# A two-layer encoder trunk in FP32 on one core: order of the down projection's loads, two banks for a broadcast, two remainders on VectorE

## Chip, cores and metric

The kernel runs on one core of a Trainium2 chip. The metric is the device time of one execution in microseconds (us); lower is better. The core has five engines with instruction streams of their own: PE (TensorE, matmuls; PEld is its weight loading), DVE (VectorE), ACT (ScalarE), POOL (GpSimd) and SP (SyncE, which here issues nearly all DMA transfers). SBUF is the on-chip memory, PSUM holds the matmuls' results in eight banks.

## The reference

The input is 1024 tokens by 1024 features. Layer 0 is an mLSTM mixer and a SwiGLU, layer 1 is chunked attention and a SwiGLU, and an RMSNorm ends it. The change touches only the two SwiGLU blocks and the last norm:

```python
def rmsnorm(x, g):
    y = x32 * lax.rsqrt(jnp.mean(x32 * x32, axis=-1, keepdims=True) + EPS) * g.astype(jnp.float32)

def swiglu(h, w_gate, w_up, w_down):
    return (jax.nn.silu(h @ w_gate) * (h @ w_up)) @ w_down
...
x = x + swiglu(rmsnorm(x, g), w_gate, w_up, w_down)
```

The hidden size of the SwiGLU is 2816, that is 22 blocks of 128. All of it is in FP32.

## The kernel before

**Precision.** Each FP32 operand is split into a high part, which ACT casts, and a remainder, which DVE or POOL subtracts (operand minus high part). A block product is three matmuls: high by high, remainder by high, high by remainder. So an operand is of use to PE only when load, cast and subtraction are done, in this order.

**Gate and up projections** (`gate_up`, product at L989). They use a Strassen-Winograd scheme: per unit n (a pair of 128-wide blocks of the gate or of the up weights) seven products a, b, c, d of sums of blocks. For each unit the weights are loaded to `wr`, DVE makes the sums s1 and s2 (L954, L959) and POOL s3 and s4 (L955, L960). `wc{layer}{n}_{c}` is the split weight of product c; its high part is L965 (ACT), its remainder L967, on POOL for unit 0 and for product 0 of unit 1, on DVE elsewhere. The input is multiplied in before its norm is known. The norm's sum of squares is built beside it: L309 adds squares into `f_s`, L316 sums over partitions on PE (`f_ps`), L278 to L285 take the reciprocal root on DVE, L332 in `finish_b` broadcasts it over the partitions on PE in two halves of four matmuls (`f_pb0`, `f_pb4`), and ACT copies each half to `f_rbc` (L341). The first results are multiplied by it (L1004, L1006, L1008) before Silu (L1007). Eight PSUM banks are split in one `mx` bank and seven `pj` banks that the products use.

**Down projection** (`down`, product at L1261, L1262 in the changed file). Seven sums i = 0 to 6 (b11, b21, t4, t3, t2, n1, b22) of the gated hidden state, stored in device memory by `gate_up`, are multiplied by four output blocks u: 28 products of 33 matmuls with 512 columns, in the order (0,0), (0,1), (0,2), (0,3), (1,0) and so on. In layer 1 the last sum is done in two halves of 256 columns (at = 0, 1). `fetch(i, k)` loads operand k of sum i through an `hr` slot (L1134, six slots) and splits it to `hc` (L174 on ACT, L175 on DVE). `prepare(i, u)` splits the weight to `wc` (two slots); for sum 0 the weight comes in three pieces `wd{layer}first...` through the same `hr` slots (L1157), for the other sums from tiles `wd` loaded whole (`wload`, L1128, 704 KB each) or combined from two of them (L1143 to L1149). The residual blocks h0 to h7 (512 KB each, L1238, L1247) are read back for `settle` (L1198 to L1222), which adds the products up. In layer 1 `scale_out` (L1184 to L1190) multiplies the finished half or quarter of the output by the last norm's factor and stores it; `fin_ps`, `fin_pb` and `fin_rbc` are that norm's sum, broadcast and copy.

**What sets the order.** The kernel is written in program order, and the order within each engine's stream follows from it and from the priorities of the operations: each engine then works its stream strictly in order. SP issues the loads in order as well; an issue waits for its slot, and for the load eight places earlier to have landed. The lines of the down projection that set the loads are these:

```python
need = [("w", 0, 0, 0)] + [("x", 0, k) for k in range(NP)] + [("w", 0, 1, 0)]
...
for u in range(NU):
    nc.sync.dma_start(h[u], mixed.kept[u])
    wload(u, 0, 1)
```

## Time and profile before

| what | us |
|---|---|
| median of 3 runs | 2446.05 |
| lowest and highest run | 2440.4, 2451.39 |
| the profiled execution, its own time | 2446.85 |
| its span in the trace | 2445.1 |
| PE busy (share of the span) | 2332.5 (95%) |
| DVE, POOL, ACT busy | 1706.7 (70%), 1029.2 (42%), 975.9 (40%) |

The span is the time between the first and the last event that the trace shows on the core; 1.75 us of the profiled execution lie outside it. Busy times are averages over stages with different limits. In brackets behind a row of a timeline stands the idle time of the engine before it, and the work that ended this idle time.

### The profile page before, as it was taken

The page shows a single profiled execution, that of the slowest core. Times are in us where ns is not written, and L with a number is a line of the kernel's source. Part 1 is how long each engine was busy: PE and PEld are TensorE (multiplying, and loading weights), DVE is VectorE, ACT ScalarE, POOL GpSimd, SP SyncE. Part 2 cuts the span into 40 slices and gives each one's busy share as a digit, 9 for nine tenths or more (in the row PEclk, how much of TensorE's full clock was granted, in tenths as well). Part 3 has the DMA queues.
Part 4 walks back from the last instruction along what each step waited for, and adds up shares of the span by engine and source line. Part 5 has one row for each costly group of instructions (what it writes and reads, how often), then busy time and mean ns, then how long its engine had stood idle before and what let it go on. Part 6 is the DMA issues. An engine that isn't in the chain of part 4 may idle for free. (4 is left out here: it accounts for less than half of the span.)

```text
span 2445.1 us, 31222 instructions
## 1 busy us (share of the span) xinstructions
PE 2332.5 (95%) x11568; PEld 1929.3 (79%) x11568; DVE 1706.7 (70%) x2699; ACT 975.9 (40%) x1826; POOL 1029.2 (42%) x644
## 2 busy tenths in 40 slices
PE   8999999989999997999999999989889999997997
PEld 7888787777888886888878787868677888876877
DVE  6544455887777765797377777787887777764887
ACT  5322222442332323544366666655533322333444
POOL 2000000476666661122664545350776666640142
PEclk9999999989999998999999999999999999998999
DMA  3110102312223227542111111001312232239431
GB/s 135 44 35 26 44 19 86 131 67 104 101 94 116 100 103 291 205 142 76 53 45 39 37 38 40 32 23 45 122 70 98 96 129 91 104 124 355 159 124 52
DMA packets 91017, 232.00 MB, mean 95 GB/s; under 512 B 10096, under 2 KB 13424, under 8 KB 90864
## 3 DMA queue, kind: packets, MB, share of 16 engines
q1 hardware_dynamic: 89136, 227.91, 26.9%
q8 instruction: 90, 1.47, 0.3%
q10 hardware_dynamic: 1728, 2.10, 0.2%
q14 instruction: 63, 0.52, 0.1%
HBM read 177.01 MB, written 52.95 MB: 94 GB/s over the span
## 5 line engine op out<-in xcount | busy, mean ns | idle before, releaser
L1261 PE MATMUL dn<-hc,wc 128*128 128x512 f32 (+1 forms) x1980 | 432.7, 380 | 27.3 <-ACT wc L174 23.9
L1261 PEld LDWEIGHTS dn<-hc,wc 128*128 128x128 f32 x1980 | 357.0, 190 | 101.8 <-ACT wc L174 24.7
L989 PE MATMUL a<-b,wc 128*128 128x512 f32 x1056 | 261.6, 398 | 8.2 <-POOL wc L967 4.2
L989 PE MATMUL c<-t,wc 128*128 128x512 f32 x1056 | 257.6, 393 | 6.2 <-DVE c L1062 6.2
L989 PEld LDWEIGHTS a<-b,wc 128*128 128x128 f32 x1056 | 201.9, 191 | 55.0 <-ACT wc L965 4.9
L989 PEld LDWEIGHTS c<-t,wc 128*128 128x128 f32 x1056 | 199.2, 189 | 51.1 <-DVE c L1062 7.5
L967 DVE TENSOR_TENSOR wc<-s,wc 128x512 fp32r<-128x512 f32 x168 | 181.4, 1081 | 68.5 <-ACT wc L965 67.3
L965 ACT CAST wc<-s 128x512 fp32r<-128x512 f32 x176 | 107.7, 619 | 183.6 <-PE d L989 111.6
L730 POOL TENSOR_TENSOR hv<-num 128x1024 f32<-128x1024 f32 x8 | 15.2, 1895 | 342.4 <-ACT num L706 342.4
L174 ACT CAST wc<-wd 128x512 fp32r<-128x512 f32 x156 | 82.0, 582 | 141.4 <-PE dn L1261 132.0
L989 PE MATMUL b<-t,wc 128*128 128x512 f32 x528 | 131.6, 399 | 6.1 <-POOL wc L967 6.1
L175 DVE TENSOR_TENSOR hc<-hr,hc 128x512 fp32r<-128x512 f32 x154 | 105.3, 728 | 36.7 <-ACT hc L174 36.6
L989 PE MATMUL d<-b,wc 128*128 128x512 f32 x528 | 131.0, 397 | 0.0
L965 ACT CAST wc<-wr 128x512 fp32r<-128x512 f32 x132 | 80.5, 618 | 125.7 <-PE c L989 42.6
L989 PE MATMUL d<-n,wc 128*128 128x512 f32 x528 | 130.6, 396 | 0.0
L967 DVE TENSOR_TENSOR wc<-wr,wc 128x512 fp32r<-128x512 f32 x124 | 113.0, 912 | 20.0 <-ACT wc L965 20.0
L1400 ACT ACTIVATE p<-p,mn 128x640 f32<-128x640 f32 (+4 forms) x128 | 89.2, 697 | 87.8 <-DVE mn L1389 80.9
L989 PEld LDWEIGHTS b<-t,wc 128*128 128x128 f32 x528 | 100.7, 191 | 29.1 <-POOL wc L967 7.0
L174 ACT CAST hc<-hr 128x512 fp32r<-128x512 f32 x154 | 89.4, 617 | 72.4 <-DMA hr<-kb 53.2
L989 PEld LDWEIGHTS d<-b,wc 128*128 128x128 f32 x528 | 99.3, 188 | 24.1
L989 PEld LDWEIGHTS d<-n,wc 128*128 128x128 f32 x528 | 100.2, 191 | 21.7
L1022 POOL TENSOR_TENSOR c<-c,c 128x512 f32<-128x512 f32 x44 | 73.1, 1662 | 104.2 <-DVE c L1066 89.9
(817 smaller groups left out, 5828.2 us busy)
## 6 DMA issues: line engine op xcount, KB each, us to landing
wd<-in_w_down_dram SPq DMA_DIRECT2D x40, 704.0 KB, 7.8
wr<-in_w_gate_dram SPq DMA_DIRECT2D x44, 512.0 KB, 4.4
wr<-in_w_up_dram SPq DMA_DIRECT2D x44, 512.0 KB, 4.3
kb<-c SPq DMA_DIRECT2D x66, 256.0 KB, 2.3
kt<-t SPq DMA_DIRECT2D x66, 256.0 KB, 2.0
hr<-kb SPq DMA_DIRECT2D x66, 256.0 KB, 4.0
hr<-kt SPq DMA_DIRECT2D x66, 256.0 KB, 3.9
hd<-h SPq DMA_DIRECT2D x16, 512.0 KB, 2.7
```

Of the source, the lines that this page charges most:

```text
L174: nc.scalar.copy(hi, src)
L175: nc.vector.tensor_tensor(lo, src, hi, ALU.subtract)
L730: nc.gpsimd.tensor_tensor(x, nv, nv, ALU.mult)
L965: hi = nc.scalar.copy(t[:, 0:HT], src)
L967: eng.tensor_tensor(t[:, HT:T], src, t[:, 0:HT], ALU.subtract)
L989: nc.tensor.matmul(ps, a, b, start=(first and k == 0 and i == 0), stop=(k == len(xs) - 1 and i == 2), skip_group_check=True,)
L1022: nc.gpsimd.tensor_tensor(x, x, g, ALU.mult)
L1261: nc.tensor.matmul(ps, a, b, start=(k == 0 and j == 0), stop=(k == NP - 1 and j == 2))
L1400: nc.scalar.activation(p, p, AF.Exp, bias=mnv, scale=-1.0, accum_out=sm)
```

## The change

It has four parts.

1. In `finish_b` the second half of the broadcast takes a `pj` bank, where the first half has the `mx` bank (when the tiles are pinned, which is so in `gate_up`).
2. The remainders of products 0 and 1 of unit 0 are subtracted on DVE, not on POOL.
3. In `down` only blocks u = 0 and 1 of sum 0 load their weights in pieces. Blocks 2 and 3 are loaded whole, once, right behind the second piece load; these tiles serve later sums too, so that two loads of 704 KB per layer fall away. The loads of h0 to h3 and of the tiles (u,0,1) move from ahead of the products into the products of sum 0, and those of h4 to h7, of (u,1,1) and of the tiles (0,0,0) and (1,0,0) into those of sum 1.
4. In layer 1 the scaling of the finished first half of the output moves from behind product (4,3) to behind (5,0), and that of the next quarter from behind (6,3) of the first half to behind the first product of the second half.

```diff
@@ -327,7 +327,7 @@
             t0, nt = cols.start // P, (cols.stop - cols.start) // P
             for i0 in range(0, nt, 4):
                 n = min(4, nt - i0)
-                pb = mxt(f"{self.name}_pb{t0 + i0}")
+                pb = (pjt if pin and i0 else mxt)(f"{self.name}_pb{t0 + i0}")
                 for i in range(n):
                     mm = nc.tensor.matmul(
                         pb[:, i * P : (i + 1) * P],
@@ -963,7 +963,7 @@
             src = (a11, s2, s3, s1, a12, a22, s4)[c]
             t = full("hl", f"wc{layer}{n}_{c}", F32R)
             hi = nc.scalar.copy(t[:, 0:HT], src)
-            eng = nc.gpsimd if n == 0 or (n, c) == (1, 0) else nc.vector
+            eng = nc.gpsimd if n == 0 and c > 1 or (n, c) == (1, 0) else nc.vector
             eng.tensor_tensor(t[:, HT:T], src, t[:, 0:HT], ALU.subtract)
             ready[n, c] = t
             return hi
@@ -1152,7 +1152,7 @@
             t = pools["wc"].tile([P, 2, WC], F32R, tag="wc", name=f"wc{layer}{i}{u}{at}")
             block = ((0, 0), (0, 1), (1, 1), (1, 0), (1, 0), (0, 0), (0, 1))[i]
             for c, n in pieces:
-                if i == 0:
+                if i == 0 and u < 2:
                     src = hrt(f"wd{layer}first{u}{c}")[:, 0:n]
                     nc.sync.dma_start(src, wsrc(u, 0, 0)[:, c : c + n])
                 else:
@@ -1228,26 +1228,27 @@
         order = [(i, u, 0) for i in range(len(names)) for u in range(NU)]
         if last:
             order += [(i, u, 1) for i, u, _ in order[-NU:]]
-        need = [("w", 0, 0, 0)] + [("x", 0, k) for k in range(NP)] + [("w", 0, 1, 0)]
-        for step in need:
-            (prepare if step[0] == "w" else fetch)(*step[1:])
+        prepare(0, 0)
+        for k in range(NP):
+            fetch(0, k)
+        prepare(0, 1)
+        for u in (2, 3):
+            wload(u, 0, 0)
         for e in range(NK):
-            ht = coret(f"hr{layer}_{e}")
-            h.append(ht)
-        for u in range(NU):
-            nc.sync.dma_start(h[u], mixed.kept[u])
-            wload(u, 0, 1)
+            h.append(coret(f"hr{layer}_{e}"))
         for m, (i, u, at) in enumerate(order):
             if m + 2 < len(order) and order[m + 2][2] == 0:
                 combine(*order[m + 2][:2])
             if m + 1 < len(order) and order[m + 1] not in wcs:
                 prepare(*order[m + 1])
             if i == 0:
-                wload(u, 0, 0)
+                wload(u, 0, 1)
+                nc.sync.dma_start(h[u], mixed.kept[u])
+            if i == 1:
                 nc.sync.dma_start(h[u + NU], mixed.kept[u + NU])
-            if i == 0 and u >= 2:
-                for v_ in (2 * u - 4, 2 * u - 3):
-                    wload(v_, 1, 1)
+                wload(u, 1, 1)
+                if u >= 2:
+                    wload(u - 2, 0, 0)
             if i == 2:
                 wload(u, 1, 0)
             w = wcs.pop((i, u, at))
@@ -1267,12 +1268,12 @@
             if i == 4:
                 wload(u, 0, 1)
             settle(i, u, at, n, ps)
-            if last and u == NU - 1:
-                if i == 4:
-                    r_fin.append(coret("fin_rbc"))
-                    scale_out(hs(0))
-                if i == 6:
-                    scale_out(slice(HT + at * n, HT + at * n + n))
+            if last and (i, u) == (5, 0):
+                r_fin.append(coret("fin_rbc"))
+                scale_out(hs(0))
+            if last and (i, u, at) in ((6, 0, 1), (6, NU - 1, 1)):
+                c = HT if u == 0 else HT + n
+                scale_out(slice(c, c + n))
         sb.close()
         return xs, st
 
```

The order on the engines at the places concerned follows. First SP at the start of the down projection of layer 1, before, from the last store of the hidden state that is needed first; `hr1_e` is residual block e, `hr11_k` operand k of sum 1, `wd1uij` a whole weight tile of block u, `wd1first2...` the pieces of block 2:

```order
L1013 DMA kt4_110_19148<-t41_10_19137 128x512
L1238 DMA hr1_1_19259<-hd11_15467 128x1024
L1238 DMA hr1_2_19260<-hd12_15570 128x1024
L1128 DMA wd1001_19267<-in_w_down_dram 128x1408
L1128 DMA wd1101_19270<-in_w_down_dram 128x1408
L1128 DMA wd1201_19273<-in_w_down_dram 128x1408
L1238 DMA hr1_3_19261<-hd13_15754 128x1024
L1128 DMA wd1301_19276<-in_w_down_dram 128x1408
L1128 DMA wd1000_19278<-in_w_down_dram 128x1408
L1247 DMA hr1_4_19262<-hd14_15889 128x1024
L1134 DMA hr11_0_19315<-kb21_10_16144 128x512
L1134 DMA hr11_1_19320<-kb21_11_16450 128x512
```

The same place after the change:

```order
L1013 DMA kt4_110_19136<-t41_10_19125 128x512
L1134 DMA hr11_0_19295<-kb21_10_16132 128x512
L1134 DMA hr11_1_19300<-kb21_11_16438 128x512
L1134 DMA hr11_2_19352<-kb21_12_16738 128x512
L1128 DMA wd1200_19246<-in_w_down_dram 128x1408
L1128 DMA wd1300_19248<-in_w_down_dram 128x1408
L1128 DMA wd1001_19258<-in_w_down_dram 128x1408
L1128 DMA wd1101_19315<-in_w_down_dram 128x1408
L1246 DMA hr1_1_19251<-hd11_15455 128x1024
L1134 DMA hr11_3_19357<-kb21_13_17038 128x512
L1128 DMA wd1201_19372<-in_w_down_dram 128x1408
L1246 DMA hr1_2_19252<-hd12_15558 128x1024
```

The operands of sum 1 and the whole tiles of blocks 2 and 3 now stand directly behind the stores, ahead of residual blocks 1 to 4 and of the tiles (u,0,1); the pieces of block 2 are gone.

PE in the gate and up projections of layer 0, where the norm's factor is broadcast (`f0_pb0` and `f0_pb4` are the two halves, `d00` and `d01` products of the two column halves), as a difference:

```order
 L332 MATMUL f0_pb0_4202<-packed_58,f00_y_4064 128x128 x4
+L332 MATMUL f0_pb4_4208<-packed_58,f00_y_4064 128x128 x4
 L989 MATMUL d01_4217<-n1_00_3630,wc01_3_4111 128x512 x3
 L989 MATMUL d01_4217<-n1_01_3733,wc01_3_4111 128x512 x3
-L989 MATMUL d01_4217<-n1_02_3836,wc01_3_4111 128x512
-L332 MATMUL f0_pb4_4208<-packed_58,f00_y_4064 128x128 x4
-L989 MATMUL d01_4217<-n1_02_3836,wc01_3_4111 128x512 x2
+L989 MATMUL d01_4217<-n1_02_3836,wc01_3_4111 128x512 x3
```

The second half of the broadcast moved up by seven matmuls, directly behind the first.

DVE at the start of the gate and up projections of layer 0, two pieces of the difference (`wc00_0` and `wc00_1` are the split weights of products 0 and 1 of unit 0):

```order
 L833 TENSOR_TENSOR h1_7_3471<-h1_7_3471,wb7_p0_3882 128x512
 L833 TENSOR_TENSOR h1_7_3471<-h1_7_3471,wb7_p1_3899 128x512
+L967 TENSOR_TENSOR wc00_0_3952<-wr00_3946,wc00_0_3952 128x512
 L898 SCALAR_TENSOR_TENSOR n1_03_3962<-h1_3_3183,packed_58,xg03_3955 128x512
 L954 TENSOR_TENSOR s1_00_3982<-wr00_3946 128x512
...
 L881 TENSOR_TENSOR t3_03_3969<-xg03_3955,t3_03_3969 128x512
 L954 TENSOR_TENSOR s1_01_4008<-wr01_3949 128x512
+L967 TENSOR_TENSOR wc00_1_3990<-s2_00_3986,wc00_1_3990 128x512
 L959 TENSOR_TENSOR s2_01_4012<-s1_01_4008,wr01_3949 128x512
 L178 SCALAR_TENSOR_TENSOR b21_00_4098<-h1_4_3244,packed_58,b21_00_4098 128x512
```

The first remainder stands ahead of the input's last block, the second between the sums s1 and s2 of unit 1. Further on in the same stream the sum s1 of unit 2 moved behind the last t4, b21 and b22 of the input.

PE at the end of the down projection of layer 1, around the last norm's first half, before (`dn1500` is product (5,0)):

```order
L1261 MATMUL dn1500_20545<-hc15_4_20397,wc1500_20410 128x512 x3
L1261 MATMUL dn1500_20545<-hc15_5_20453,wc1500_20410 128x512 x2
L316 MATMUL fin_ps0_20491<-ones_59,fin_s_19176 128x1 x4
L1261 MATMUL dn1500_20545<-hc15_5_20453,wc1500_20410 128x512
L1261 MATMUL dn1500_20545<-hc15_6_20458,wc1500_20410 128x512 x3
L1261 MATMUL dn1500_20545<-hc15_7_20463,wc1500_20410 128x512 x3
L1261 MATMUL dn1500_20545<-hc15_8_20468,wc1500_20410 128x512 x3
L332 MATMUL fin_pb0_20512<-packed_58,fin0_y_20500 128x128 x4
L1261 MATMUL dn1500_20545<-hc15_9_20473,wc1500_20410 128x512 x3
```

And after the change (`dn1510` is product (5,1)):

```order
L1262 MATMUL dn1500_20474<-hc15_10_20454,wc1500_20386 128x512 x3
L316 MATMUL fin_ps0_20523<-ones_59,fin_s_19164 128x1 x4
L1262 MATMUL dn1510_20577<-hc15_0_20251,wc1510_20467 128x512 x3
...
L1262 MATMUL dn1510_20577<-hc15_6_20434,wc1510_20467 128x512 x3
L332 MATMUL fin_pb0_20544<-packed_58,fin0_y_20532 128x128 x4
L1262 MATMUL dn1510_20577<-hc15_7_20439,wc1510_20467 128x512 x3
```

The sum moved from within product (5,0) to its end, and the broadcast from there into (5,1).

## Rows read from the trace of the kernel before

**Rows 1.** The profile's page: its first line, and of its list of the costliest groups the matmuls of the down projection (line engine op out<-in xcount | busy us, mean ns of one | idle us of the engine just before them, what ended most of it).
```profile
span 2445.1 us, 31222 instructions
...
L1261 PE MATMUL dn<-hc,wc 128*128 128x512 f32 (+1 forms) x1980 | 432.7, 380 | 27.3 <-ACT wc L174 23.9
```

**Rows 2.** The timeline of PE (TensorE) at the start of the down projection of layer 1 (two rows) and of layer 0 (two rows). Columns: start us, us, engine line op out<-in, form, count, and in brackets the idle time before and what ended it. The windows end at 2260 and 1000 us, so the second row of each pair goes on behind them.
```profile
2195.22 15.16 PE L1261 MATMUL dn<-hc,wc 128*128 128x512 f32 x65 [1.15 <-DVE wc L175]
2222.72 37.55 PE L1261 MATMUL dn<-hc,wc 128*128 128x512 f32 x151 [12.33 <-ACT wc L174]
...
937.58 15.18 PE L1261 MATMUL dn<-hc,wc 128*128 128x512 f32 x65 [1.15 <-DVE wc L175]
964.29 35.90 PE L1261 MATMUL dn<-hc,wc 128*128 128x512 f32 x146 [11.53 <-ACT wc L174]
```

**Rows 3.** Windows at the same two places, in the order layer 1 (three rows) and layer 0 (two): window, length, busy us and count of PE, PEld, DVE, ACT and POOL, PE's granted clock (1.00 is full speed), busy share of the DMA engines, GB/s.
```profile
2210.40:2222.70 12.30, 0.00 (x0) 0.00 (x0) 2.06 (x4) 2.46 (x5) 0.00 (x0) 0.67 1.02 408
2222.70:2226.00 3.30, 3.28 (x7) 2.36 (x8) 1.79 (x3) 1.01 (x2) 0.00 (x0) 0.50 1.02 396
2226.00:2230.00 4.00, 4.00 (x14) 3.15 (x14) 2.42 (x4) 2.90 (x5) 0.00 (x0) 0.72 1.04 402
964.30:968.00 3.70, 3.70 (x8) 2.68 (x9) 1.77 (x3) 0.99 (x2) 0.00 (x0) 0.50 1.01 392
968.00:972.00 4.00, 4.00 (x17) 3.21 (x17) 2.24 (x4) 2.69 (x5) 0.00 (x0) 0.91 1.06 406
```

**Rows 4.** The timeline of SP's DMA issues at the start of the down projection of layer 1 (start us, us of issuing, line, destination<-source, count). hd are the kept residual blocks, kb the stored sums of the gated hidden state, wd and wd1first weights.
```profile
2201.84 0.88 SPq L1238 DMA_DIRECT2D hr<-hd  x2
2202.77 1.40 SPq L1128 DMA_DIRECT2D wd<-in_w_down_dram  x3
...
2204.80 1.06 SPq L1128 DMA_DIRECT2D wd<-in_w_down_dram  x2
2206.12 0.53 SPq L1247 DMA_DIRECT2D hr<-hd  x1
2208.21 2.60 SPq L1134 DMA_DIRECT2D hr<-kb  x2
2212.23 3.35 SPq L1157 DMA_DIRECT2D wd1first<-in_w_down_dram  x3
```

**Rows 5.** The timelines of ACT (two rows) and of DVE (one row) in the same stretch.
```profile
2220.64 1.30 ACT L174 CAST hc<-hr 128x512 fp32r<-128x512 f32 x2 [9.63 <-DMA hr<-kb]
2222.05 1.66 ACT L174 CAST wc<-wd1first 128x512 fp32r<-128x512 f32 x3
...
2200.17 2.85 DVE L175 TENSOR_TENSOR wc<-wd1first,wc 128x512 fp32r<-128x512 f32 x3
```

**Rows 6.** The list of DMA issues in the window 2160 to 2300 us: destination<-source, queue, count, KB each, median us from issue to landing.
```profile
wd<-in_w_down_dram SPq DMA_DIRECT2D x16, 704.0 KB, 8.4
...
hr<-kb SPq DMA_DIRECT2D x22, 256.0 KB, 4.7
```

**Rows 7.** The timeline of PE in the gate and up projections: layer 0 (four rows), layer 1 (two rows).
```profile
489.06 7.94 PE L989 MATMUL a<-b,wc 128*128 128x512 f32 x23 [2.08 <-POOL wc L967]
...
499.93 4.10 PE L989 MATMUL b<-t,wc 128*128 128x512 f32 x11 [2.70 <-POOL wc L967]
...
524.88 2.08 PE L332 MATMUL f_pb<-packed,f_y 128*128 128x128 f32 x8 [5.28 <-ACT f_rbc L341]
...
562.10 4.14 PE L989 MATMUL c<-t,wc 128*128 128x512 f32 x10 [2.92 <-DVE c L1062]
...
1782.10 2.08 PE L332 MATMUL f_pb<-packed,f_y 128*128 128x128 f32 x8 [5.33 <-ACT f_rbc L341]
...
1820.04 3.04 PE L989 MATMUL c<-t,wc 128*128 128x512 f32 x12 [2.58 <-DVE c L1062]
```

**Rows 8.** The timelines of POOL (two rows), DVE (three) and ACT (one) at the start of the gate and up projections of layer 0.
```profile
498.62 1.25 POOL L967 TENSOR_TENSOR wc<-s,wc 128x512 fp32r<-128x512 f32 x1
...
529.11 1.75 POOL L1004 TENSOR_TENSOR c<-c,f_rbc 128x512 f32<-128x512 f32 x1
...
499.90 0.69 DVE L959 TENSOR_TENSOR s<-s,wr 128x512 f32<-128x512 f32 x1 [2.37 <-POOL wc L967]
...
510.60 0.69 DVE L967 TENSOR_TENSOR wc<-wr,wc 128x512 fp32r<-128x512 f32 x1
...
527.92 1.77 DVE L959 TENSOR_TENSOR s<-s,wr 128x512 f32<-128x512 f32 x1
...
527.24 0.57 ACT L341 COPY f_rbc<-f_pb 128x512 f32<-128x512 f32 x1
```

**Rows 9.** One window of the gate and up projections of layer 0, columns as in the windows above.
```profile
530.00:540.00 10.00, 10.00 (x45) 8.13 (x45) 9.78 (x10) 3.85 (x7) 9.92 (x7) 1.00 0.07 28
```

**Rows 10.** The timelines of PE (four rows) and of DVE (one) at the end of the down projection of layer 1. fin_ps and fin_pb are the sums and the broadcast of the last norm.
```profile
2367.26 1.02 PE L316 MATMUL fin_ps<-ones,fin_s 128*128 128x1 f32 x8 [1.70 <-DVE fin_s L309]
2368.15 4.13 PE L1261 MATMUL dn<-hc,wc 128*128 128x512 f32 x10
...
2383.50 32.47 PE L1261 MATMUL dn<-hc,wc 128*128 128x512 f32 x212 [1.17 <-DVE wc L175]
...
2421.07 0.68 PE L332 MATMUL fin_pb<-packed,fin_y 128*128 128x128 f32 x4 [0.60 <-DVE fin_y L285]
...
2373.82 6.63 DVE L1187 SCALAR_TENSOR_TENSOR hr<-hr,packed,fin_rbc 128x512 f32<-128x512 f32 x5 [2.34 <-ACT fin_rbc L341]
```

## The prediction

> **What bounds the kernel now.** I read the page first, then PE's timeline for its idle places, then at each place the streams of the engine or queue that ended the wait. PE is the bound over the whole span; its idle time is small and sits in a few places. Of 27.3 us of idle time in the down projection, 23.9 lie in two waits ended by the cast of a weight [rows 1]: 12.33 us in layer 1 and 11.53 in layer 0, each two products after the start, where block 2 of sum 0 is due [rows 2]. In the wait PE runs nothing and the DMA engines run full at 408 GB/s [rows 3]. SP shows why: three residual blocks and five whole weight tiles go out before the first operand of sum 1 at 2208.21 and the pieces of block 2 at 2212.23 [rows 4], and ACT casts what it had waited for only at 2220.64 and 2222.05 [rows 5]. So this is an order of loads, not a lack of DMA rate: the tiles sent first are wanted only from sum 1 on. After each wait PE's granted clock is .50 and then .72 (layer 1) or .91 (layer 0) before it is full again [rows 3]: .50 of 2.4 GHz is the lower of its two levels, and what came before was an idle PE.
>
> **Part 3, the down projection.** Removed are the two waits and what the clock costs behind them. Layer 1: 3.3 us at .50 and 4.0 at .72 lose 3.3 x .50 + 4.0 x .28 = 2.8 us; layer 0: 3.7 x .50 + 4.0 x .09 = 2.2 [rows 3]. Together 12.33 + 2.8 + 11.53 + 2.2 = 28.9 us [rows 2, 3].
>
> What is late next? After the change three operands (256 KB each) and then the tile of block 2 (704 KB) go out at about 2201.8, when the residual blocks went out before [rows 4]. With the last stores in flight I take 1.77 MB ahead of and including that tile: 1.77 MB / .398 MB per us (between the rates of 396 and 408 in rows 3) is 4.4 us, and 1.4 us for issue and landing make 2207.6. The first third of the weight then needs a cast (1.66 us for three [rows 5], .6 for one) and a subtraction (.69 [rows 8]): 2208.9. Block 2 is due at the end of product (0,1), 2210.4 [rows 2]. So no wait by 1.5 us, which is thin. The other end is what the first operand of sum 1 took in this very place, issued at 2208.21 and cast at 2220.64, 12.4 us [rows 4, 5]: a tile issued at 2201.8 would land at 2214.2, be ready at 2215.6, and PE would wait 5.2 us and lose about 1 on its clock, 6.3 per layer. I take 1 us per layer, near the lower end, because the 12.4 us had over 5 MB ahead of them (five tiles and three residual blocks sent in the 4.3 us before [rows 4]), and medians in this stretch are 8.4 us for such a tile and 4.7 for an operand [rows 6].
>
> Sum 1 is next. A product of 33 matmuls is 7.6 us (two of them, but for the first matmul, take 15.16 [rows 2]), so sum 0 ends at about 2225.5 and the last operand of (1,0) is due at 2232.4. By then 9.04 MB must be in (1.77, and behind them five tiles, three residual blocks and eight operands): 22.7 us at .398 from 2201.8, plus 2.7 for landing and splitting, give 2227.2; slack 5 us. It fails only below some .32 MB per us, and the lowest rate in rows 3 is .39. The two tiles that are saved (1.44 MB) are 3.6 us of queue in the same stretch. Residual blocks 1 to 3 are behind them; `settle` wants them on ACT and DVE, not on PE, and with six `pj` banks a late one has some products of cover. Blocks 4 to 7 now wait for an SBUF slot that an operand of sum 0 holds until about 2225.5, and SP's whole queue waits with the first of them; behind it are the operands of sum 2, due at 2255.8. Cover 30 us, price nothing unless that slot comes free much later (rival 4). Net: 28.9 - 2 = **26.9 us**, bounds 16.3 and 28.9.
>
> **Part 4, the tail.** PE waits 1.70 us for the last addition of the statistics, runs ten matmuls in 4.13 us where rows 2 give .233 each (2.3 us), so 1.8 on the clock, waits 1.17 for a weight's remainder that DVE makes behind 6.63 us of scaling, and .60 at the quarter [rows 10]; 5.3 us in all. The sum moved behind the whole product has 5 us more cover. The scaling now lies in product (5,1) or later and can push another remainder back in the same way; I leave 1.5 us for that: **3.8 us**, bounds 0 and 5.3. The end itself, behind the last matmul, isn't touched.
>
> **Parts 1 and 2, gate and up.** On PE's stream they look large. Its second matmul waits 2.08 us for a remainder on POOL; DVE stands idle there and could give it 1.8 earlier. The next wait is 2.70 us [rows 7], for POOL's L967 at 498.62 [rows 8]; on DVE it stands behind s1 and ends at about 498.2, so that PE is some 1.7 us earlier behind both. The second half of the broadcast waits 5.28 us (5.33 in layer 1) for ACT's copy of the first, from which its bank comes free [rows 7]; with a bank of its own this wait goes. In full 1.7 + 5.3 = 7.0 per layer.
>
> But PE is not the bound in what follows. DVE is busy 9.78 of 10 us and POOL 9.92 in 530 to 540 [rows 9], and PE waits again at 562.10 (2.92 us) and 1820.04 (2.58 us) for DVE's L1062 [rows 7], since banks come free only at the pace of those two. PE's gain counts as far as their chain moves up. Of DVE's stream the wait of 2.37 us for POOL at 499.90 goes [rows 8], and a remainder of .69 comes in ahead; the sum s1 of unit 2 (about 1.8 beside POOL) goes behind the last t4, so that t4, the copies of the broadcast (the second at 527.24) and POOL's first multiplication (529.11) come earlier [rows 8]. POOL loses two subtractions. Bounds: 0, if the saturated pair takes as long as before, and 7.0. I take 2.5 per layer, near DVE's 2.37 less .69 plus part of s1: **5 us** in both.
>
> Row 8 also shows a price of running both: a DVE subtraction takes .69 us at 510.60, with POOL idle, and 1.77 at 527.92, beside POOL's 529.11 and the one before it [rows 8]. The Trainium skill, page "SBUF — State Buffer", section "Who interferes with whom", says that a DVE instruction with two SBUF inputs and a GpSimd instruction that reads SBUF exclude each other, and the later one blocks until the first is done. The trace agrees in kind: the slow one takes about the sum of both. By that rule a subtraction moved from POOL to DVE frees nothing where both are full, which is rival 1.
>
> **The rivals.**
> 1. DVE and POOL together are one resource in 510 to 550: parts 1 and 2 only lengthen the waits at 562.10 and 1820.04 by what they save ahead. For it rows 8 and 9; against it that both added subtractions stand ahead of 500, where DVE is idle 2.37 us. Gate and up give 0: 2410 + 5 = 2415.
> 2. The contrary: banks come free early enough, 7.0 per layer. Against it rows 7 and 9. 2410 - 9 = 2401.
> 3. The moved tile lands late, a wait of 5.2 us stays at block 2. 6.3 - 1 = 5.3 more per layer: 2421.
> 4. Slower: blocks 4 to 7 wait for a slot, and SP is in order. If the slot came free not with sum 0 (2225.5) but with sum 1 (2255.8), the operands of sum 2, queued behind, would begin to be ready 12.4 us after [rows 4, 5], the last of the eleven (2.88 MB at .398) 7.2 later: PE would wait up to 19.6 us per layer, with 2.5 on the clock, 44 in all: 2455. It decides from a release after about 2238; the slot is of an operand of sum 0, which speaks against it.
> 5. The change doesn't do what it says: the queue is so full that the waits only move from block 2 to sum 1, and parts 1, 2 and 4 alone count: 2446.85 - 3.8 - 5 = 2438.
>
> **How the numbers follow.** Against the profiled execution's own 2446.85 (span 2445.1 [rows 1]): 26.9 + 3.8 + 5 = 35.7 gives 2411.1. That execution lies .8 us above the median of the runs, so the forecast is 2410 (2411.1 - .8 = 2410.3). Chances: forecast .50, rival 1 .17, rival 2 .10, rival 3 .13, rival 4 .04, rival 5 .06. The range 2400 to 2422 takes in the first four cases, .90 with sharp edges, some .80 with the spread of each. About .5% (12 us) is what a measurement can tell from no change: the first four lie below 2434, so faster .90; rival 5 is within, .06; rival 4 slower, .04.
>
> **What would show it.** In the down projection: no wait of over 2 us between products (0,1) and (0,2), PE's granted clock at 1.00 through sum 0, operands of sum 1 landed before 2225 on this scale, and SP's issue of block 4 at the end of sum 0. If a wait stays there, rival 3; if it stands at (1,0), rival 5; at (2,0), rival 4. In gate and up: both halves of the broadcast back to back, no wait for L341, and the wait for L1062 longer than now by what was saved (rival 1), or gone (rival 2). In the tail: no wait ahead of `fin_ps`, and one of at most a microsecond for a remainder behind the scaling. The forecast is wrong if the down projection gives less than 16 us, or if a new wait of over 5 us shows anywhere.

## The result

The changed kernel takes 2412.15 us (median of four runs, 2410.46 to 2422.65) against 2445.78 us before: 33.6 us less, a ratio of 0.9871 with an interval of 0.9836 to 0.9907. The forecast was 2410 with a range of 2400 to 2422. A second group of runs gave 2414.30 us and a ratio of 0.9867 (0.9851 to 0.9884).

The profile's page of the changed kernel first: its first line and two of the costliest groups.

```profile
span 2408.7 us, 31190 instructions
...
L1262 PE MATMUL dn<-hc,wc 128*128 128x512 f32 (+1 forms) x1980 | 427.0, 377 | 3.2 <-DVE wc L175 2.8
...
L989 PE MATMUL c<-t,wc 128*128 128x512 f32 x1056 | 258.8, 395 | 19.2 <-DVE c L1062 19.2
```

The idle time ahead of the down projection's matmuls fell from 27.3 us [rows 1] to 3.2. That ahead of product c of the gate and up projections, for DVE's L1062, is now 19.2 us; before, its waits were 2.92 and 2.58 [rows 7] and one of .70. So the profile shows at once where the gain came from and where another gain was lost.

PE's timeline at the start of the down projection, layer 1 (three rows), then layer 0 (two rows):

```profile
2176.82 15.16 PE L1262 MATMUL dn<-hc,wc 128*128 128x512 f32 x65 [1.16 <-DVE wc L175]
2192.27 0.51 PE L1262 MATMUL dn<-hc,wc 128*128 128x512 f32 x1 [0.29 <-ACT wc L174]
2193.00 52.24 PE L1262 MATMUL dn<-hc,wc 128*128 128x512 f32 x227 [0.22 <-DVE wc L175]
...
949.65 0.50 PE L1262 MATMUL dn<-hc,wc 128*128 128x512 f32 x1 [0.20 <-ACT wc L174]
950.38 49.94 PE L1262 MATMUL dn<-hc,wc 128*128 128x512 f32 x217 [0.22 <-DVE wc L175]
```

The rows that answer to the waits of 12.33 and 11.53 us [rows 2] have .29 and .20 us, and as much again ahead of the second matmul. Below are ACT's cast of the moved tile of block 2, SP's issue of residual block 4, and two windows (columns as in rows 3):

```profile
2191.60 1.55 ACT L174 CAST wc<-wd 128x512 fp32r<-128x512 f32 x3 [2.79 <-DMA wd<-in_w_down_dram]
...
2205.67 0.38 SPq L1248 DMA_DIRECT2D hr<-hd  x1
...
2185.00:2200.00 15.00, 14.48 (x63) 11.33 (x62) 7.52 (x12) 5.97 (x12) 0.00 (x0) 1.00 1.02 399
2200.00:2215.00 15.00, 15.00 (x67) 12.33 (x66) 9.18 (x16) 7.82 (x15) 0.00 (x0) 1.00 1.00 376
```

On the forecast's scale, counted from the first matmul of the stage (2193.68 before, 2175.27 now), the tile's cast starts at +16.33; the forecast had its landing at +13.9 (2207.6) and the deadline at +16.7 (2210.4). The tile came 2.4 us later than reckoned, and 1.5 of slack plus .5 of waiting covered nearly all of that. So the place is tight: the forecast's slack is used up. Block 4 is issued at 2205.67, at the end of sum 0, as forecast. The DMA engines go on full, at 399 and 376 GB/s, and PE's granted clock is 1.00 in both windows, where it was .50 and .72 after the wait [rows 3].

The gate and up projections on PE, layer 0 (four rows) and layer 1 (one):

```profile
485.14 5.65 PE L989 MATMUL a<-b,wc 128*128 128x512 f32 x23 [0.96 <-DVE wc L967]
...
495.97 4.93 PE L989 MATMUL b<-t,wc 128*128 128x512 f32 x11 [4.04 <-DVE wc L967]
...
513.53 1.95 PE L332 MATMUL f_pb<-packed,f_y 128*128 128x128 f32 x16
...
558.89 4.50 PE L989 MATMUL c<-t,wc 128*128 128x512 f32 x12 [9.61 <-DVE c L1062]
...
1801.52 4.40 PE L989 MATMUL c<-t,wc 128*128 128x512 f32 x12 [9.61 <-DVE c L1062]
```

Both halves of the broadcast stand back to back (16 matmuls at 513.53), and no wait for L341 is left, where there were 5.28 and 5.33 us [rows 7]. The wait for L1062 grew to 9.61 in both layers. The wait for the second remainder did not shrink: 4.04 us in place of 2.70 [rows 7]; PE only came to it earlier, and left it 12.3 us into the stage (495.97) where it had been 13.4 (499.93).

The end of the down projection of layer 1: PE (four rows), DVE (three) and POOL (one), and then the same three operations of DVE before the change:

```profile
2337.86 1.05 PE L316 MATMUL fin_ps<-ones,fin_s 128*128 128x1 f32 x8 [1.29 <-DVE fin_s L309]
2338.78 5.07 PE L1262 MATMUL dn<-hc,wc 128*128 128x512 f32 x21
2343.68 1.06 PE L332 MATMUL fin_pb<-packed,fin_y 128*128 128x128 f32 x8
2344.49 37.61 PE L1262 MATMUL dn<-hc,wc 128*128 128x512 f32 x243
...
2333.24 1.78 DVE L1209 TENSOR_TENSOR hr<-hr,v 128x512 f32<-128x512 f32 x1
2334.95 2.25 DVE L175 TENSOR_TENSOR wc<-wd,wc 128x512 fp32r<-128x512 f32 x2
2337.13 0.68 DVE L309 TENSOR_TENSOR fin_s<-fin_s,fin_q 128x512 f32<-128x512 f32 x1
...
2332.80 3.39 POOL L1212 TENSOR_TENSOR hr<-hr,v 128x512 f32<-128x512 f32 x2 [7.04 <-DVE v L1208]
```

```profile
2364.76 0.68 DVE L1209 TENSOR_TENSOR hr<-hr,v 128x512 f32<-128x512 f32 x1
2365.36 1.15 DVE L175 TENSOR_TENSOR wc<-wd,wc 128x512 fp32r<-128x512 f32 x2
2366.44 0.68 DVE L309 TENSOR_TENSOR fin_s<-fin_s,fin_q 128x512 f32<-128x512 f32 x1
```

A wait of 1.29 us for the statistics stays where 1.70 stood [rows 10]; the matmuls behind it lose little (21 in 5.07 us), and the wait of 1.17 us is gone: 37.61 us without an idle place.

The stages, as differences between PE's first matmuls of each (in us; the last runs to the end of the span):

| stage | before | changed |
|---|---|---|
| up to the first gate and up projection | 486.49 | 483.68 |
| gate and up, layer 0 | 449.54 | 449.05 |
| down, layer 0, then attention | 807.65 | 793.60 |
| gate and up, layer 1 | 450.00 | 448.94 |
| down, layer 1, and the end | 251.42 | 233.43 |

The first line isn't touched by the change: over all thirteen profiles of this study it lies between 483.1 and 486.9, with and without the change, so that its 2.8 us are chance.

The two lines of gate and up differ by .5 and 1.1 us, which one profile can't tell. Over all profiles these stages take 449.8 us on average without parts 1 and 2 (ten stages, 448.8 to 450.5) and 449.1 with them (eight stages, 448.7 to 449.7; the kernels with another order on DVE, e4_early and those made from it, are left out).

### The profile page after: what moved, and what is told of

It is laid out like the page before. It is cut to its first block, busy times and chain, and to the rows that moved or that the text cites. A ratio compares the mean times of both kernels' runs of the same rounds, so it can differ in the third digit from the quotient of the medians.

```text
span 2408.7 us, 31190 instructions
## 1 busy us (share of the span) xinstructions
PE 2321.8 (96%) x11568; PEld 1921.3 (80%) x11568; DVE 1716.3 (71%) x2703; ACT 974.1 (40%) x1826; POOL 1010.9 (42%) x640
## 5 line engine op out<-in xcount | busy, mean ns | idle before, releaser
L1262 PE MATMUL dn<-hc,wc 128*128 128x512 f32 (+1 forms) x1980 | 427.0, 377 | 3.2 <-DVE wc L175 2.8
L989 PE MATMUL c<-t,wc 128*128 128x512 f32 x1056 | 258.8, 395 | 19.2 <-DVE c L1062 19.2
L967 DVE TENSOR_TENSOR wc<-s,wc 128x512 fp32r<-128x512 f32 x170 | 187.3, 1104 | 68.4 <-ACT wc L965 67.3
L174 ACT CAST wc<-wd 128x512 fp32r<-128x512 f32 x168 | 89.1, 581 | 153.0 <-PE dn L1262 124.1
L967 DVE TENSOR_TENSOR wc<-wr,wc 128x512 fp32r<-128x512 f32 x126 | 118.2, 938 | 18.2 <-ACT wc L965 18.1
L175 DVE TENSOR_TENSOR wc<-wd,wc 128x512 fp32r<-128x512 f32 x168 | 118.0, 742 | 10.8 <-ACT wc L174 10.5
L1022 POOL TENSOR_TENSOR c<-c,c 128x512 f32<-128x512 f32 x44 | 73.1, 1662 | 104.9 <-DVE c L1066 90.6
```

The costliest lines, as they stand in the source:

```text
L174: nc.scalar.copy(hi, src)
L175: nc.vector.tensor_tensor(lo, src, hi, ALU.subtract)
L967: eng.tensor_tensor(t[:, HT:T], src, t[:, 0:HT], ALU.subtract)
L989: nc.tensor.matmul(ps, a, b, start=(first and k == 0 and i == 0), stop=(k == len(xs) - 1 and i == 2), skip_group_check=True,)
L1022: nc.gpsimd.tensor_tensor(x, x, g, ALU.mult)
L1262: nc.tensor.matmul(ps, a, b, start=(k == 0 and j == 0), stop=(k == NP - 1 and j == 2))
```

## The experiments

Eleven kernels ran, one of them the changed kernel again. Each was timed against the kernel before on the same chip; PE's "restart" below is the first matmul of product (2,5) of the gate and up projections, which waits for L1062, counted from the first matmul of that stage (75.2 us in both layers of the changed kernel; 75.6 and 76.4 before).

**e1_loads: part 3 alone.** The hunks of the diff in `prepare` and around the loads of `down`, and nothing else:

```diff
-                if i == 0:
+                if i == 0 and u < 2:
...
+        for u in (2, 3):
+            wload(u, 0, 0)
...
             if i == 0:
-                wload(u, 0, 0)
+                wload(u, 0, 1)
+                nc.sync.dma_start(h[u], mixed.kept[u])
```

> The kernel before with part 3 alone (order and number of the down projection's loads). Theory: the two waits of 12.33 and 11.53 us and the clock behind them were an order of loads, so this part alone gives 27 to 29 us (ratio about 0.988 to 0.989) and PE shows under 1 us of waits at the start of each down projection. Rival: it needs the earlier arrival at the down projection or other parts to hide the tile of block 2, then 5 us per layer of a wait stay there and it gives about 17 us.

Measured: 2418.13 against 2447.51 us, ratio 0.9880 (0.9866 to 0.9893), 29.4 us. The waits at block 2 are .19 us in layer 0 and 1.76 in layer 1, with .23 more behind it, so that "under 1 us" held in one layer only. The rival falls. The wait of 1.76 shows that the cover is thin, as the forecast had it.

**e6_order: the order of part 3 without its saving.** Parts of the loads' new place are in the diff below; blocks 2 and 3 come in pieces as before, and their whole tiles once more in sum 1:

```diff
+            if i == 0:
+                wload(u, 0, 1)
+                nc.sync.dma_start(h[u], mixed.kept[u])
+            if i == 1:
+                nc.sync.dma_start(h[u + NU], mixed.kept[u + NU])
+                wload(u, 1, 1)
+                if u >= 2:
+                    for v_ in (2 * u - 4, 2 * u - 3):
+                        wload(v_, 0, 0)
```

> The kernel before with the order of part 3 alone: block 2 and 3 of sum 0 still come in pieces, and their whole tiles again in sum 1, so that no byte is saved. Theory of the order: the two waits of 11.5 and 12.3 us go down to under 2 us each and the kernel gets 22 to 28 us faster. Rival, the bytes: the 1.44 MB per layer (3.6 us of the queue) are what made it work, and without them a wait of 3 to 4 us stays in each layer, at block 2 or at sum 1.

Measured: 2416.90 against 2446.41 us, ratio 0.9873 (0.9851 to 0.9894), 29.5 us. At the start of the down projection PE shows no wait behind the first product's own 1.15 us, in either layer. The order alone gives the whole gain, as far as intervals of some 5 us to each side can tell.

**e7_bytes: the saving without the order.**

```diff
         for u in range(NU):
             nc.sync.dma_start(h[u], mixed.kept[u])
             wload(u, 0, 1)
+        for u in (2, 3):
+            wload(u, 0, 0)
```

(and `if i == 0 and u < 2` in `prepare`, the load of (u,0,0) in sum 0 for u < 2 only)

> The kernel before with the saving of part 3 alone: blocks 2 and 3 are loaded once as whole tiles, but behind the residual blocks and the tiles (u,0,1), where the pieces stood. Theory of the order: the tile of block 2 lands late, and 5 to 8 of the 12 us of each wait stay; 8 to 14 us faster in all. Rival, the bytes: the two loads fewer are enough, the wait falls below 2 us, and it gets over 20 us faster.

Measured: 2440.44 against 2446.41 us, ratio 0.9974 (0.9964 to 0.9984), 6.0 us. PE's timeline at block 2 of layer 0 and of layer 1:

```profile
962.21 38.01 PE L1264 MATMUL dn<-hc,wc 128*128 128x512 f32 x157 [9.14 <-ACT wc L174]
...
2217.18 43.12 PE L1264 MATMUL dn<-hc,wc 128*128 128x512 f32 x177 [9.35 <-ACT wc L174]
```

The waits stay at 9.14 and 9.35 us: 2.4 and 3.0 less than in rows 2, near the 3.6 us that two tiles are in the queue. More of them stayed than I had expected (5 to 8), the gain is below the 8 to 14 us expected, and the rival of the bytes falls all the more.

**e2_tail: part 4 alone.** The last hunk of the diff:

```diff
-            if last and u == NU - 1:
...
+            if last and (i, u) == (5, 0):
+                r_fin.append(coret("fin_rbc"))
+                scale_out(hs(0))
+            if last and (i, u, at) in ((6, 0, 1), (6, NU - 1, 1)):
```

> The kernel before with part 4 alone (the scaling of the first half and of a quarter later). Theory: the tail from the first wait for the last norm's sum to the end gets 3 to 4 us shorter (ratio about 0.9985), since the wait of 1.70 us, the lower clock behind it and the wait of 1.17 us go or shrink. Rival: the later scaling crowds the end, and the stores at the end take back what the sum gives, 0 us in all.

Measured: 2446.68 against 2447.51 us, ratio 0.9992 (0.9983 to 1.0002), which allows a gain of 4 us and none. The profile still has a wait of 1.61 us for the statistics. From the profiles with part 3: the last stage, less its waits at block 2, takes 236.2 and 236.3 without part 4 (e1_loads, e6_order) and 232.8 to 234.7 with it (the changed kernel twice, e4_early, e8_early_pool, e10_pool3; mean 233.5). So part 4 gives 2.7 us there, from two profiles against five that differ among themselves by 1.9.

**e3_gate: parts 1 and 2 alone.** The first two hunks of the diff:

```diff
-                pb = mxt(f"{self.name}_pb{t0 + i0}")
+                pb = (pjt if pin and i0 else mxt)(f"{self.name}_pb{t0 + i0}")
...
-            eng = nc.gpsimd if n == 0 or (n, c) == (1, 0) else nc.vector
+            eng = nc.gpsimd if n == 0 and c > 1 or (n, c) == (1, 0) else nc.vector
```

> The kernel before with parts 1 and 2 alone (second bank for the broadcast, two remainders on DVE). Theory: PE's first waits shrink by 7 us per layer, the wait for the bank that L1062 frees grows by as much, so that the gate and up projections of each layer get only 0.4 to 1.1 us shorter and the kernel 1 to 2 us (ratio 0.9992 to 0.9996). Rival: the small gain in the changed kernel was taken by an interplay with the other parts, and alone they give the 5 us of the forecast or more.

Measured: 2446.96 against 2447.51 us, ratio 0.9997 (0.9987 to 1.0006); the stages are 449.49 and 449.70 us long, with restarts at 74.97 and 75.16. The mechanism of the theory holds; the stages are only .05 and .3 us shorter than before, less than it said, and .7 per layer over all profiles, as it said. The two layers tell more: in layer 0 PE was at the sum over partitions (`f_ps`) after 14.94 us, in layer 1 after 17.00, and yet the restarts differ by .2. Layer 0 lost its 2 us on the way, at waits of .72 and 1.06 us (.45 in layer 1) and at a granted clock of .66 behind them, and then waited 8.00 us for L1062, layer 1 9.61. The restart is not set by when PE gets there.

**e4_early: DVE's order at the wait.** The changed kernel, with the four differences n1, t2, t3, t4 of the first pair of units made behind the freeing sum. In DVE's stream of the changed kernel, that sum (L1062, 558.15) is the last row of DVE here; the rows of POOL follow (the first six rows of DVE and the first four of POOL are spoken of further below):

```profile
483.66 1.43 DVE L967 TENSOR_TENSOR wc<-wr,wc 128x512 fp32r<-128x512 f32 x1 [1.26 <-ACT wc L965]
485.01 1.77 DVE L898 SCALAR_TENSOR_TENSOR n<-h,packed,xg 128x512 f32<-128x512 f32 x1
...
494.17 1.74 DVE L967 TENSOR_TENSOR wc<-s,wc 128x512 fp32r<-128x512 f32 x1
496.01 0.69 DVE L959 TENSOR_TENSOR s<-s,wr 128x512 f32<-128x512 f32 x1
...
505.65 1.22 DVE L283 TENSOR_TENSOR f_t<-f_y 128x8 f32<-128x8 f32 x1
...
509.88 0.17 DVE L283 TENSOR_TENSOR f_t<-f_y 128x8 f32<-128x8 f32 x1
...
552.53 0.69 DVE L1033 TENSOR_TENSOR n<-c,v 128x512 f32<-128x512 f32 x1 [1.15 <-POOL v L1022]
553.26 1.63 DVE L1035 TENSOR_TENSOR t<-c,n 128x512 f32<-128x512 f32 x1
554.82 1.75 DVE L967 TENSOR_TENSOR wc<-s,wc 128x512 fp32r<-128x512 f32 x1
556.48 0.68 DVE L1057 TENSOR_TENSOR v<-b,cp 128x512 f32<-128x512 f32 x1
557.09 1.15 DVE L967 TENSOR_TENSOR wc<-wr,wc 128x512 fp32r<-128x512 f32 x1
558.15 0.68 DVE L1062 TENSOR_TENSOR c<-c,v 128x512 f32<-128x512 f32 x1
...
483.26 1.27 POOL L309 TENSOR_TENSOR f_s<-f_s,f_q 128x512 f32<-128x512 f32 x1 [1.20 <-ACT f_q L304]
484.50 1.74 POOL L955 TENSOR_TENSOR s<-wr 128x512 f32<-128x512 f32 x1
...
493.66 1.71 POOL L955 TENSOR_TENSOR s<-wr 128x512 f32<-128x512 f32 x1
...
505.55 1.30 POOL L967 TENSOR_TENSOR wc<-s,wc 128x512 fp32r<-128x512 f32 x1
...
550.92 1.58 POOL L1022 TENSOR_TENSOR v<-v,v 128x512 f32<-128x512 f32 x1 [1.29 <-DVE v L1080]
```

DVE waits 1.15 us for POOL's L1022, then runs L1033, L1035 and a remainder, then the sum L1057, another remainder, and only then L1062. PE had finished the product that L1062 adds some 14 us before (product c of unit 2 ends ahead of 544).

```diff
+            if p == 0:
+                later.append((p, x))
+            else:
+                mixes(p, x)
...
-            tt(c22, c, v, ALU.add)
+            add = tt(c22, c, v, ALU.add)
+            if n == 2:
+                with tc.issue_after(add.ins):
+                    mixes(*later.pop())
```

> The changed kernel, with the differences n1, t2, t3 and t4 of the first pair of units made after the sum of unit 2 that frees PE's bank (L1062 ahead of L1033 and L1035 on DVE). Theory of the order: PE's wait of 9.61 us in each gate and up projection is DVE's stream, in which the sum that frees the bank stands behind two operations that wait for POOL; with them behind it the wait falls to 4 to 6 us and the kernel gets 6 to 10 us faster than the changed one. Rival, the throughput of DVE and POOL: they are full, so the wait of 9.61 only moves to the next bank, and the sum of PE's waits in each gate and up projection stays within 1 us.

Measured: 2411.17 against 2447.51 us, ratio 0.9853 (0.9838 to 0.9868). PE at the restart in layers 0 and 1:

```profile
557.80 4.62 PE L989 MATMUL c<-t,wc 128*128 128x512 f32 x12 [4.49 <-DVE c L1070]
...
1797.38 4.61 PE L989 MATMUL c<-t,wc 128*128 128x512 f32 x12 [4.23 <-DVE c L1070]
```

The wait fell to 4.49 and 4.23 us and the restart came at 71.5 and 71.8, as the theory of the order had it: the wait isn't throughput alone. The rival falls too: PE's idle times in the stage, with the one ahead of its first matmul, add up to 11.6 and 10.9 us, against 17.7 in both layers of the changed kernel. But the gain is smaller than I had said (6 to 10). The stages are 445.76 and 448.04 us long, 3.3 and .9 less than in the changed kernel, so 2.8 and 5.9 us of what the waits lost came back elsewhere in PE's stage, where is not settled; in layer 1 two waits of .56 and .71 for the same line come later. By the ratios it is 3.4 us faster than the changed kernel (0.9853 and 0.9867), with intervals that overlap. The stages show the gain when more profiles are taken: 446.8 us on average with this order (e4_early, e8_early_pool, e11_both; 445.8 to 448.0), 448.9 without it (the changed kernel twice, e9_tail51; 448.7 to 449.0), so 2.2 per layer; e10_pool3 below, which moves more work to POOL as well, has no such gain. The times don't settle it.

**e8_early_pool: both remainders on POOL again.** e4_early with the old rule for the remainders' engine:

```diff
-            eng = nc.gpsimd if n == 0 and c > 1 or (n, c) == (1, 0) else nc.vector
+            eng = nc.gpsimd if n == 0 or (n, c) == (1, 0) else nc.vector
```

> The changed kernel with the four differences of the first pair of units behind the freeing sum, as in the fourth run, and without part 2: both remainders on POOL again. Theory: on DVE the two remainders took 1.43 and 1.74 us beside POOL where .69 was reckoned, and this pushes DVE's whole chain; with them on POOL product (2,5) restarts 1 to 2 us earlier, at 69.5 to 70.5 us after the first matmul of the stage (71.5 and 71.8 in the fourth run). Rival: POOL is as full as DVE, its chain sets the same end, and the restart stays within 0.5 us of 71.6 or comes later.

Measured: 2412.41 against 2446.41 us, ratio 0.9861 (0.9845 to 0.9878). Restarts at 72.7 and 72.9, later and not earlier: the theory falls, and the rival holds. The stages take 446.54 and 446.72 us, as in e4_early on average (446.90), so which of the two engines has these remainders makes no difference that can be seen.

**e10_pool3: three more remainders on POOL.** e4_early, with products 4, 5 and 6 of unit 1 on POOL:

```diff
-            eng = nc.gpsimd if n == 0 and c > 1 or (n, c) == (1, 0) else nc.vector
+            eng = nc.gpsimd if n == 0 and c > 1 or n == 1 and c in (0, 4, 5, 6) else nc.vector
```

> The fourth kernel (differences of the first pair behind the freeing sum), with the remainders of products 4, 5 and 6 of unit 1 on POOL, which stands idle for 4.5 us there, in place of DVE, where they take .69 us each. Theory of two resources: DVE's chain loses 2.1 us, POOL has room, and product (2,5) restarts about 2 us earlier than in the fourth run, at 69 to 70 us after the first matmul of the stage. Rival, one resource: POOL's three subtractions hold up DVE's operations beside them by about 1.1 us each, so the restart stays at 71.5 or comes later, up to 73.

Measured: 2411.36 against 2447.51 us, ratio 0.9852 (0.9832 to 0.9873). Restarts at 73.35 and 73.34, 1.5 to 1.9 later than in e4_early: the rival holds, with .3 more than its 73. The stages are 448.49 and 450.09 us long, 2.7 and 2.1 more than in e4_early, though the times of the two kernels are equal (2411.36 and 2411.17). PE's restart in layer 0, two rows of DVE and one of POOL:

```profile
560.28 5.49 PE L989 MATMUL c<-t,wc 128*128 128x512 f32 x12 [4.21 <-DVE c L1070]
...
511.12 1.20 DVE L284 SCALAR_TENSOR_TENSOR f_t<-f_t,f_v 128x8 f32<-128x8 f32 x1
...
512.76 0.17 DVE L284 SCALAR_TENSOR_TENSOR f_t<-f_t,f_v 128x8 f32<-128x8 f32 x1
...
509.79 2.50 POOL L967 TENSOR_TENSOR wc<-wr,wc 128x512 fp32r<-128x512 f32 x2
```

DVE was spared 2.1 us of its own work (three times .69), and by the later restart got more than that back in waiting: even an operation on 128 x 8 elements (L284) takes 1.20 us while POOL is at a subtraction, and .17 when it isn't. The order of two sums for unit 2 moved a little too (s1 earlier on DVE, s3 earlier on POOL), so the 1.5 to 1.9 us aren't the price of the three subtractions alone.

**e9_tail51: the scaling one product later.** The changed kernel with one line different:

```diff
-            if last and (i, u) == (5, 0):
+            if last and (i, u) == (5, 1):
```

> The changed kernel with the scaling of the first half moved one product further, behind (5,1). Theory: in the changed kernel the last norm's sum still waits 1.3 to 1.6 us, because DVE's last addition to the statistics stands behind two remainders of the weight of (5,1) and is no further ahead of the sum than before; one product later the wait is gone, with the lower clock behind it, and the tail gets 1.3 to 3 us shorter. Rival: the wait is of the addition's input from the product itself and moves along, or the scaling then delays a weight at a later product by as much: tail within 0.5 us.

Measured: 2416.36 against 2447.51 us, ratio 0.9875 (0.9854 to 0.9896); the last stage less its wait at block 2 is 235.0 us, no shorter than with the changed kernel (232.9 and 234.7). PE's timeline at the end:

```profile
2343.59 0.95 PE L316 MATMUL fin_ps<-ones,fin_s 128*128 128x1 f32 x8
...
2349.81 1.16 PE L332 MATMUL fin_pb<-packed,fin_y 128*128 128x128 f32 x8 [0.33 <-DVE fin_y L285]
...
2368.27 15.70 PE L1262 MATMUL dn<-hc,wc 128*128 128x256 f32 x131 [1.29 <-DVE wc L175]
```

The wait for the sum is gone, as the theory had it. But a wait of 1.29 for a weight's remainder is back at 2368.27, behind the scaling, as it was before the change (1.17 [rows 10]). The rival's second half holds.

**e11_both and e5_after.** The first has the edits of e4_early and of e9_tail51, the second is the changed kernel once more, without an edit.

> The changed kernel with the differences of the first pair behind the freeing sum (fourth run) and the scaling behind (5,1). Theory: the gains add up, 3 to 5 us from the gate and up projections and 1.3 to 3 from the tail, 4 to 8 us faster than the changed kernel (ratio to the kernel before 0.983 to 0.985). Rival: the earlier end of one stage is lost at the next one's loads, and it stays within 2 us of the changed kernel.

Measured: 2413.62 against 2447.51 us, ratio 0.9861 (0.9841 to 0.9882). The gate and up projections are 446.58 and 446.93 us long, 2.5 and 2.0 less than in the changed kernel; the tail gives nothing. By the ratios (0.9861, and 0.9867 and 0.9871 for the changed kernel) the total is some 2 us below the changed kernel's, so the expected 4 to 8 us did not come.

> The changed kernel once more, beside the other kernels of this group. All theories: ratio 0.985 to 0.988, and its profile as the first one: product (2,5) of the gate and up projections restarts 75.2 us after the first matmul of that stage.

Measured: 2414.30 against 2446.41 us, ratio 0.9867; restarts at 74.6 and 75.2.

## Why the prediction was right, and where it wasn't

The total was right: 35.7 us were forecast from the profiled execution, 33.6 measured between the medians. The mechanism of the largest term was right; two smaller terms were too large, and for gate and up rival 1 was nearer than the forecast. That the total came within 2.1 us is in part luck: a down projection that gave 2.5 us more than forecast stands against a tail that gave 1 to 2 less and gate and up that gave 3.4 less.

**Down projection: 26.9 us forecast, 29.4 (26.2 to 32.8) measured alone.** That the wait is an order of loads is shown by e6_order (all of the gain with all the bytes) and e7_bytes (6 us with fewer bytes). The forecast lies within the interval, so that the term isn't shown to be low; if it is, two things fit. I took off 1 us per layer, and the waits that stayed are .4 and .5 us in the changed kernel, 2.0 at most in one layer of e1_loads. And the waits of the kernel before differ between executions: 12.34 and 13.56 us in e2_tail, 11.90 and 13.71 in e3_gate, where loads are as before, against 11.53 and 12.33 in the one trace that I reckoned from. One number of the working was short: 5.8 us from the issue of the first operand to the tile's landing (4.4 for 1.77 MB, and 1.4 for issue and landing, for which no row was given) came out as 8.2, from 2183.43 to the cast at 2191.60. Rivals 3, 4 and 5 fall: .5 us of waiting stay at block 2 and not 5.2, the slot of block 4 comes free with sum 0, and no wait is at sum 1.

**Tail: 3.8 us forecast, 2 to 2.7 measured** (e2_tail by its ratio, and the stages). The step that failed is "the sum moved behind the whole product has 5 us more cover". The sum moved from behind matmul 17 of product (5,0) to behind matmul 33, which is 16 matmuls or 3.7 us at the .233 of rows 2, and DVE's last addition moved as well: counted from the start of product (5,0), at 2361.50 before and 2328.86 now, its end went from +5.6 (2367.12) to +9.0 (2337.81), 3.3 us later. So only .4 of the wait of 1.70 went, and 1.29 stayed. Of the 3.3, some 2.2 are DVE's operations beside POOL's L1212: 1.78 us for L1209 and 2.25 for two remainders, where they took .68 and 1.15 before; the other 1.1 is that DVE came to them later. What the rest of the term gave depends on the clock: of the 5.3 us, 1.9 stay in the changed kernel's profile (1.29, .2 on the clock, .41 at the quarter) and 3.8 in e5_after's (1.64, 1.8, .41). The second part of the step, that the scaling can push a remainder back, is shown by e9_tail51.

**Gate and up: 5 us forecast, 1.6 measured** (.5 and 1.1 in the stages; .9 and 1.0 in e5_after; 1.3 over all profiles). The bounds held, and rival 1 (0) was nearer than my 2.5 per layer. The step that failed is "the wait of 2.37 us for POOL at 499.90 goes, and a remainder of .69 comes in ahead". The wait went, but the two remainders took 1.43 and 1.74 us on DVE: the first met the end of POOL's L309 (483.26 to 484.53), the second that of s3 (L955, 493.66 to 495.37), and L898 behind the first took 1.77 beside the s3 at 484.50. Counted from the first matmul of the stage, DVE's next sum L959 starts at +12.3 (496.01) where it stood at +13.4 (499.90): 1.1 us earlier, where 1.7 and a part of s1 were reckoned, and PE restarts .4 and 1.2 us earlier.

The broadcast gave nothing that can be seen. PE had its second half behind it 7.7 us earlier, counted from the start of the stage, and waits that off at the end, 9.61 us. In e4_early the first half comes 27.7 us into the stage in layer 0 and 32.5 in layer 1, and the restarts are .3 us apart. Part 1 alone wasn't run; but part 2 alone, which is all that e4_early and e8_early_pool differ by, moves the restart by 1.2 and 1.1 us, as much as both parts do over all profiles (75.6 to 76.4 in ten stages without them, 74.6 to 75.2 in eight with them).

The prediction's own signs say the same: a wait for L1062 that is longer by what was saved was its sign for rival 1. A new wait of over 5 us was its sign of being wrong; 9.61 us stand at a place that had waits before, but 7 us of them are new, and for this term the sign was right. Rival 2 (7.0 per layer) falls with this wait.

Rival 1 gave the throughput of DVE and POOL as the reason. That is half of it. It is shown that work moved between the two changes little (e8_early_pool) or harms (e10_pool3), which is what one would expect if the two exclude each other. The Trainium skill, page "SBUF — State Buffer", section "Who interferes with whom", states such an exclusion for DVE operations with two SBUF inputs and POOL operations that read SBUF; the trace agrees, with 1.43 and 1.74 us beside POOL against .69 without it. The prediction's "about the sum of both" is too much, though: an operation of DVE that meets one of POOL takes what is left of POOL's and then some .6 more, as the first remainder, which ends at 485.09 behind POOL's 484.53. But it is shown as well that the wait isn't this alone: with the same work in another order, PE restarts 3.5 us earlier (e4_early). The sum that frees the bank stood behind operations that waited for POOL and that nobody needed then. How much of the 9.61 us is left to be had stays open: later waits for the same line appear when the first is shortened, and the four kernels with the new order are 1 to 5 us faster than the changed one by their ratios (0.9852 to 0.9861 against 0.9867 and 0.9871), within what the times can tell.

## What to carry to other kernels

When a queue is full and its customer waits, look first at what stands ahead of the late load and when that is wanted: putting the loads in the order of need gave 29 us here without saving a byte, and saving bytes without the order gave 6. A wait removed from an engine that isn't the bound of its stage came back here, nearly whole, at the next buffer that the bound engines free; before costing such an edit, find that buffer and what stands ahead of the freeing operation in its engine's stream. And cost an operation that is moved to DVE by what it takes beside the operations that POOL will run at that moment, not by its time alone.

## What the runs showed of the hardware that was not expected

Tiny DVE operations can pay nearly the whole price of a POOL operation beside them: L283 on 128 x 8 elements took 1.22 us at 505.65, beside POOL's subtraction at 505.55, and .17 at 509.88 with POOL idle (rows of e4_early's section, from the changed kernel). Whoever reckons such a chain by its alone times is off by up to about a microsecond for each operation that meets POOL.

After nearly equal waits for the statistics at the end the granted clock wasn't the same. PE in e4_early (two rows) and in e8_early_pool (two rows):

```profile
2336.66 1.05 PE L316 MATMUL fin_ps<-ones,fin_s 128*128 128x1 f32 x8 [1.23 <-DVE fin_s L309]
2337.57 5.06 PE L1273 MATMUL dn<-hc,wc 128*128 128x512 f32 x21
...
2336.86 1.05 PE L316 MATMUL fin_ps<-ones,fin_s 128*128 128x1 f32 x8 [1.24 <-DVE fin_s L309]
2337.77 6.68 PE L1273 MATMUL dn<-hc,wc 128*128 128x512 f32 x21
```

Behind 1.23 us (e4_early) the next 21 matmuls took 5.06 us at a granted clock of 1.00, behind 1.24 us (e8_early_pool) 6.68 at .73. So a wait of this length may cost 1.6 us more or not, which alone makes two groups of the tail's length (the last stage less its waits at block 2): 232.8 to 232.9 us in three profiles with part 4 as it stands, 234.3 and 234.7 in two.
